# The second MLP of a decoder trunk in one written order on four engines, and the weight sums of the first MLP tied to its rows

## The chip, the cores and the metric

One NeuronCore of one Trainium2 chip runs the whole program. The metric is device time in microseconds (us) from launch to end of one execution, median over runs. Engines: TensorE (PE in the profile, PEld its weight loads), VectorE (DVE), ScalarE (ACT), GpSimd (POOL), and SyncE (SP), which issues loads.

## The reference, cut to what matters

Two layers work on 272 tokens (16 meta tokens and 256 others) of width 2048. Layer 0 mixes with RWKV-7, layer 1 with gated linear attention (GLA); after each stands a squared-ReLU MLP with 8192 hidden columns:

```python
def sq_relu_mlp(x, w1, w2):
    h = jax.nn.relu(x @ w1)
    return (h * h) @ w2
# in each layer i
h = h + mix_out                      # RWKV-7 (i = 0) or GLA (i = 1)
h = h + sq_relu_mlp(rms_norm(h, norm_mlp[i]), mlp_w1[i], mlp_w2[i])
# at the end
return rms_norm(h, norm_f)[:, N_META:]
```

All data are float32. The kernel computes each large product in three passes: a weight tile `raw` is split into `hi` (a rounded copy, by ScalarE) and `lo = raw - hi` (by VectorE), the activations likewise, and hi·hi, hi·lo and lo·hi are accumulated.

## The kernel before

The program is one straight line of stages: RWKV, the first MLP (`mlp`), GLA, the second MLP (`mlp1`). Where nothing else is said, a scheduler places each engine's instructions at compile time, by its own estimate of when their inputs are ready and by a priority; on the chip each engine then runs its list strictly in that order. `manual_schedule(engines=...)` instead puts the listed engines' instructions in the order in which the program states them. `high_priority(offset=2000)` lets the scheduler pull an instruction ahead of others.

**First MLP** (`mlp`, layer 0). The hidden columns come in 4 blocks (`NHB`) of 2048. `up(b)` makes 16 rows of 128 hidden columns, `down(b)` adds 16 rows of 128 output columns; `up(1)` runs before `down(0)`, and so on: 128 rows. A row is two weight tiles of 128x1024 (512 KB), each loaded by SP (L134), split by ScalarE (L142) and VectorE (L143), and used by 24 matmuls (L165 to L167). Three `raw` buffers and two `hi`/`lo` pairs.

**The weight sums** (`differences`). The second MLP's down product forms most of its 2x2-block products by seven products instead of eight (Strassen in Winograd's form), for six of the eight pairs of hidden rows (`FAST`). That wants three sums of weight quarters, made ahead of time: for each of 48 units (4 blocks, 2 halves of the output columns, 6 pairs) GpSimd fetches three 128x512 quarters into free `x` tiles (L329), VectorE forms three sums (L334 to L336), GpSimd stores them to the DRAM tensor `diff` (L342). The 51 steps are called between the rows of `mlp` (`paced`), store of unit u-3, fetch of u, sums of u-2 in each; nothing in the data ties a step to its row.

**Second MLP** (`mlp1`). For each block b: rows (`up`, 16 of them, two weight tiles each, 16 times a 512-wide and a 256-wide matmul, L405 and L406, into a PSUM bank `own[0]`, in a few rows another), and units (`down(b, g)`, g = output half, 8 pairs p each). A fast unit loads three tiles: A (two quarters), B (two stored sums), E (a quarter and a sum); VectorE makes a fourth, half-size operand A - B (`raw4`, L490), and seven products of three matmuls follow (L448 to L450). The two other pairs load two tiles and do eight products. After a row, ScalarE and VectorE join the two halves of the bank (L208, L209), apply the squared ReLU (L409, L414), form four sums `F` for fast pairs, and split the result into `HS` or `HC` (L426, L427). After p = 6 and p = 7 the seven banks are added into `htok`. PE's order is written by hand: rows and units alternate; VectorE, ScalarE and SP go by the scheduler, loads and splits at high priority. There are five `raw` buffers and four `hi`/`lo` pairs:

```python
def load(parts):                       # L368
    with tc.high_priority(offset=2000):
        raw = self.t(pool, [P, 1024], "raw", self.raw_bufs if pool is self.wp else 2)
        for to, src in parts:
            nc.sync.dma_start(raw[:, to], src)
        return split(pool, raw, 1024)  # L377: ScalarE cast L380, VectorE subtract through tt, L356
```

All of `mlp1`'s VectorE tensor-tensor operations show as L356 (the helper `tt`); the tiles tell them apart.

Of the kernel before, what the change touches and what calls it, by code (L numbers as in the profile page):

```python
# [56 lines left out]
class Kern:  # L57
# [203 lines left out]
    def mlp(self, layer, x, rstd, hres, off, done):  # L261
# [3 lines left out]
        with ExitStack() as es:  # L265
            hp = es.enter_context(tc.tile_pool(name=f"hid{layer}", bufs=1, side="right", reuse_waits="tile"))

            def up(b):
                hid = []
                for f in range(KT):  # L270
# [23 lines left out]
            pre = iter(())  # L294
            if layer == 0:
                pre = self.paced(self.differences(), 2 * NHB * KT - 8)
# [11 lines left out]
    def paced(self, steps, n):  # L308
        steps = list(steps)
        done = 0  # L310
        for i in range(n):
            while done < (i + 1) * len(steps) // n:
                steps[done]()
                done += 1
            yield

    def differences(self):
# [3 lines left out]
        held = {}  # L321

        def fetch(u):
            b, g, i = units[u]
            w = self.operands(b, g, FAST[i])
            held[u] = [self.t(self.xp, [P, 2, T], "x", KT, F32R).bitcast(F32).rearrange("p s t -> p (s t)")[:, :512]
                       for _ in range(3)]
            for x, k in zip(held[u], (0, 3, 2)):
                nc.gpsimd.dma_start(x, w[:, k])  # L329

        def form(u):
            x11, x12, x22 = held[u]
            tt = nc.vector.tensor_tensor
            tt(out=x22, in0=x22, in1=x12, op=ALU.subtract)  # L334
            tt(out=x12, in0=x12, in1=x11, op=ALU.subtract)
            tt(out=x11, in0=x11, in1=x22, op=ALU.add)  # L336

        def store(u):
            b, g, i = units[u]
            t2, t1, t3 = held.pop(u)  # L340
            for x, k in ((t1, 0), (t3, 1), (t2, 2)):
                nc.gpsimd.dma_start(self.diff[b, g, i][:, k], x)  # L342

        def step(u):
            if u >= 3:
                store(u - 3)
            if u < len(units):
                fetch(u)
            if 2 <= u < len(units) + 2:
                form(u - 2)  # L350

        return [lambda u=u: step(u) for u in range(len(units) + 3)]

    def mlp1(self, x, rstd):
        nc, tc, ap = self.nc, self.tc, self.ap
        tt = lambda o, a, b, op: nc.vector.tensor_tensor(out=o, in0=a, in1=b, op=op)  # L356
        w1, hres, rs = ap["mlp_w1_1"], self.hres, rstd[:, :SEQ]
# [5 lines left out]
        tmp = [flat[:, D + 512 * i : D + 512 * i + 512] for i in range(4)]  # L363
        ssq = self.t(hp, [P, 2, 4], "ssq")
        sum3 = self.t(hp, [P, 2], "sum3")
        pools = [self.wp, hp]

        def load(parts):  # L368
            with tc.high_priority(offset=2000):
                pool = pools.pop(0)  # L370
                pools.append(pool)
                raw = self.t(pool, [P, 1024], "raw", self.raw_bufs if pool is self.wp else 2)
                for to, src in parts:
                    nc.sync.dma_start(raw[:, to], src)
                return split(pool, raw, 1024)

        def split(pool, raw, n):  # L377
            hi = self.t(pool, [P, n], "hi" if n == 1024 else "hi4", self.hi_bufs, F32R)
            lo = self.t(pool, [P, n], "lo" if n == 1024 else "lo4", self.hi_bufs, F32R)
            nc.scalar.copy(hi, raw)  # L380
            tt(lo, raw, hi.bitcast(F32), ALU.subtract)
            return raw, hi, lo
# [3 lines left out]
        hid, parts = {}, {}  # L386

        def turn(i):
# [5 lines left out]
            nc.scalar.copy(htok[:, t, 512 * q : 512 * q + 512], pt)  # L394

        def up(b, f, at=0):
            ps = own[at]
            wide, one = ps.rearrange("p (s t a) -> p s t a", s=2, a=2), self.pairs(ps[:, :SEQ])
            for i in range(2):
                hi, lo = load([(slice(0, 1024), w1[b * KT + f, i])])[1:]  # L400
                for j in range(8):
                    kt = 8 * i + j
                    ws = slice(j * P, (j + 1) * P)
                    xt = x[kt][:, :, :SEQ].rearrange("p s (a t) -> p s t a", a=2)
                    nc.tensor.matmul(wide, hi[:, ws], xt, start=kt == 0, stop=False)  # L405
                    nc.tensor.matmul(one, lo[:, ws], xt[:, 0], start=False, stop=kt == KT - 1)  # L406
            c = self.joined(hp, (self.back(ps[:, :SEQ]), self.back(ps[:, SEQ:])))
            z = self.t(hp, [P, SEQ], "z", 2)
            nc.vector.scalar_tensor_tensor(out=self.two(z), in0=c, scalar=0.0, in1=self.two(rs), op0=ALU.max, op1=ALU.mult)  # L409
            p, k = f // 2, f % 2  # L410
            if k == 0:
                parts[p] = self.t(hp, [P, 8, P], "F", 2)
            F = parts[p]
            nc.scalar.activation(F[:, 2 * k : 2 * k + 2].rearrange("p a t -> p (a t)"), z, AF.Square)  # L414
            if k == 0:
                return
            x21, x11, x22, x12, s1, s2, s3, s4 = (F[:, i] for i in range(8))
            if p in FAST:
                tt(s1, x21, x22, ALU.add)
                tt(s3, x11, x21, ALU.subtract)  # L420
                tt(s2, s1, x11, ALU.subtract)
                tt(s4, x12, s2, ALU.subtract)
                src, H = F[:, 1:], self.t(hp, [P, 2, 7, P], "HS", len(FAST), F32R)
            else:
                src, H = F[:, :4], self.t(hp, [P, 2, 4, P], "HC", KT // 2 - len(FAST), F32R)
            nc.scalar.copy(H[:, 0], src)  # L426
            tt(H[:, 1], src, H[:, 0].bitcast(F32), ALU.subtract)  # L427
            hid[p] = H

        def final(t, q, late=False):  # L430
            h, i = htok[:, t, 512 * q : 512 * q + 512], q
            sq = self.t(hp, [P, 512], "fsq", 2)
            nc.scalar.activation(sq, h, AF.Square, accum_out=ssq[:, t, i : i + 1])
# [3 lines left out]
        one, two, both = slice(0, 512), slice(512, 1024), slice(0, 1024)  # L437
        t1, u2, u3, u4 = tmp
        add = lambda o, a, c: tt(o, a, c, ALU.add)

        def down(b, g):
            C = {(t, f): htok[:, t, 1024 * g + 512 * f : 1024 * g + 512 * f + 512] for t in range(2) for f in range(2)}
            begun = set()
            end = b == NHB - 1

            def product(at, X, hi, lo, ws, last, first=False):
                wh, wl, o = self.weave(hi[:, ws]), self.weave(lo[:, ws]), self.pairs(own[at])
                nc.tensor.matmul(o, X[0], wh, start=first or at not in begun, stop=False)  # L448
                nc.tensor.matmul(o, X[0], wl, start=False, stop=False)  # L449
                nc.tensor.matmul(o, X[1], wh, start=False, stop=last)  # L450
                begun.add(at)

            def evacuate(i):
                if i == 1:
                    nc.scalar.copy(t1, own[1])
                elif i == 6:
                    add(u2, own[6], t1)
                elif i == 7:
                    add(u3, own[7], u2)
                elif i == 5:  # L460
                    add(u4, own[5], u2)
                    add(C[0, 1], own[5], C[0, 1])
                elif i == 0:
                    add(C[0, 1], own[0], C[0, 1])
                    if end and g == 1 and p == KT // 2 - 1:
                        final(0, 3, True)
                elif i == 2:
                    add(C[1, 0], own[2], C[1, 0])
                    if end and g == 1:
                        final(1, 2, True)  # L470
                elif i == 3:
                    add(C[1, 1], own[3], C[1, 1])
                    if end and g == 1:
                        final(1, 3, True)
                elif i == 4:
                    add(C[0, 0], own[4], C[0, 0])
                    if end and g == 1:
                        final(0, 2, True)

            for p in range(KT // 2):  # L480
                w, H = self.operands(b, g, p), hid[p]
                if p in FAST:
                    d = self.diff[b, g, FAST.index(p)]
                    op = lambda i: (H[:, 0, i], H[:, 1, i])
                    A = load([(both, w[:, :2])])
                    B = load([(both, d[:, 1:])])
                    E = load([(one, w[:, 2]), (two, d[:, 0])])
                    with tc.high_priority(offset=2000):
                        r4 = self.t(hp, [P, 512], "raw4", 1)
# [1187 lines left out]
```

## Time and profile before

| | before |
|---|---|
| runs | 2631.57, 2612.95, 2621.63 us |
| median | 2621.63 us |
| the profiled execution | 2621.7 us, its span 2619.9 us |
| busy in the span | PE 2413.9, PEld 2239.0, DVE 1832.4, ACT 1335.9, POOL 167.9 us |
| moved by DMA | 550.93 MB, mean 210 GB/s |
| mean granted TensorE clock | 0.967 |

The stages in the span: RWKV to about 605 us, first MLP to about 1397, GLA to 1786, second MLP to 2606, then the final norm and the output. A row of a stretch of time gives, after its length, the busy time (and instructions begun) of PE, PEld, DVE, ACT and POOL, the granted clock, the DMA engines' mean busy share and GB/s. A row of a wait gives total us, how often, and the longest. A row of a group of instructions gives count, busy time and mean ns of one, then the idle time before them. A timeline row gives start, duration, engine, line and tiles.

### The profile page before, as it was taken

Reading aid. Unit: us, or ns where it says so; the run is one execution under the profiler, and the core shown is the slowest. Engines: PE = TensorE matmul, PEld = TensorE weight load, DVE = VectorE, ACT = ScalarE, POOL = GpSimd, SP = SyncE. Lnnn points to the kernel's source line nnn. Section 1 sums busy time; section 2 is a strip of 40 time slices with the busy share of each in tenths; the row PEclk is TensorE's granted clock in tenths of the full one; section 3 lists DMA queues with packets and bytes.
Section 4 is the critical chain, followed back from the end, with each engine's and each line's share of the span. In section 5 each row is a group of like instructions: output and inputs, shape, how many; then the busy total and the mean of one; then the engine's idle time right before and its main releaser. Section 6 shows DMA issues by size and latency. Waiting matters only on the chain. (4 is left out here: it accounts for less than half of the span.)

```text
span 2619.9 us, 48317 instructions
## 1 busy us (share of the span) xinstructions
PE 2413.9 (92%) x19205; PEld 2239.0 (85%) x19205; DVE 1832.4 (70%) x3025; ACT 1335.9 (51%) x2075; POOL 167.9 (6%) x325
## 2 busy tenths in 40 slices
PE   9999999988887999999999999999888888979887
PEld 8888887887777999999999999998777777868765
DVE  8779869587766555555567777776676766766767
ACT  6477455554333345344355555555554445545544
POOL 0000000024555000000000000000000000000000
PEclk9999999998999999999999999999998989989899
DMA  6478745379999655555566555555656646656564
GB/s 210 154 234 281 220 137 160 88 248 351 393 391 382 229 190 191 189 192 187 192 200 206 178 168 163 171 200 199 198 198 199 202 165 215 200 182 196 186 209 159
DMA packets 194178, 550.93 MB, mean 210 GB/s; under 512 B 40160, under 2 KB 55776, under 8 KB 193824
## 3 DMA queue, kind: packets, MB, share of 16 engines
q1 hardware_dynamic: 170912, 472.33, 54.6%
q0 software_dynamic: 23040, 75.52, 7.8%
q8 instruction: 150, 2.46, 0.4%
q14 instruction: 76, 0.62, 0.1%
HBM read 493.89 MB, written 52.17 MB: 208 GB/s over the span
## 5 line engine op out<-in xcount | busy, mean ns | idle before, releaser
L142 ACT CAST hi<-raw 128x1024 fp32r<-128x1024 f32 (+1 forms) x562 | 526.2, 947 | 638.8 <-PE pj L166 494.4
L143 DVE TENSOR_TENSOR lo<-raw,hi 128x1024 fp32r<-128x1024 f32 (+1 forms) x562 | 613.2, 1100 | 286.5 <-ACT hi L142 282.6
L167 PE MATMUL pj<-x,lo 128*128 128x272 f32 (+1 forms) x2560 | 727.4, 284 | 59.8 <-DVE lo L143 59.6
L165 PE MATMUL pj<-x,hi 128*128 128x272 f32 (+1 forms) x2560 | 737.7, 288 | 4.6 <-DVE r L566 3.9
L166 PE MATMUL pj<-x,hi 128*128 128x272 f32 (+1 forms) x2560 | 723.0, 282 | 1.4 <-DVE x L242 1.4
L167 PEld LDWEIGHTS pj<-x,lo 128*128 128x128 f32 x2560 | 493.5, 193 | 69.0 <-DVE lo L143 68.5
L165 PEld LDWEIGHTS pj<-x,hi 128*128 128x128 f32 x2560 | 493.6, 193 | 17.9 <-issue 9.8
L380 ACT CAST hi<-raw 128x1024 fp32r<-128x1024 f32 (+1 forms) x352 | 339.3, 986 | 313.7 <-DVE raw L356 82.5
L166 PEld LDWEIGHTS pj<-x,hi 128*128 128x128 f32 x2560 | 493.7, 193 | 4.2 <-DVE x L242 1.6
L356 DVE TENSOR_TENSOR lo<-raw,hi 128x1024 fp32r<-128x1024 f32 (+1 forms) x352 | 394.5, 1148 | 130.0 <-ACT hi L380 129.0
L405 PE MATMUL pj<-x,hi 128*128 128x512 f32 x896 | 323.0, 406 | 46.4 <-DVE cj L209 29.5
L165 PE MATMUL pj<-h,hi 128*128 128x272 f32 x1024 | 285.8, 279 | 1.0 <-ACT hi L142 1.0
L167 PE MATMUL pj<-h,lo 128*128 128x272 f32 x1024 | 285.9, 279 | 0.8 <-DVE lo L143 0.8
L166 PE MATMUL pj<-h,hi 128*128 128x272 f32 x1024 | 285.7, 279 | 0.0
L406 PE MATMUL pj<-x,lo 128*128 128x256 f32 x896 | 257.0, 287 | 5.1 <-DVE lo L356 4.9
L405 PEld LDWEIGHTS pj<-x,hi 128*128 128x128 f32 x896 | 180.6, 202 | 80.8 <-ACT hi L380 29.9
L165 PEld LDWEIGHTS pj<-h,hi 128*128 128x128 f32 x1024 | 193.5, 189 | 1.2 <-ACT hi L142 1.2
L167 PEld LDWEIGHTS pj<-h,lo 128*128 128x128 f32 x1024 | 193.5, 189 | 1.1 <-DVE lo L143 1.0
L166 PEld LDWEIGHTS pj<-h,hi 128*128 128x128 f32 x1024 | 193.5, 189 | 0.0
L406 PEld LDWEIGHTS pj<-x,lo 128*128 128x128 f32 x896 | 182.6, 204 | 11.2 <-DVE lo L356 10.1
L342 POOL DMA_DIRECT2D diff<-x x144 | 78.3, 545 | 534.6 <-DVE x L334 464.4
L329 POOL DMA_DIRECT2D x<-w_d x144 | 77.9, 542 | 129.7 <-DMA diff<-x 56.4
(369 smaller groups left out, 3583.8 us busy)
## 6 DMA issues: line engine op xcount, KB each, us to landing
raw<-mlp_w_d SPq DMA_DIRECT2D x384, 512.0 KB, 4.4
raw<-gla_in_d SPq DMA_DIRECT2D x98, 512.0 KB, 3.8
raw<-w_rkv_d SPq DMA_DIRECT2D x80, 512.0 KB, 4.3
raw<-w_d SPq DMA_DIRECT2D x80, 512.0 KB, 4.8
x<-w_d POOLq DMA_DIRECT2D x144, 256.0 KB, 7.7
diff<-x POOLq DMA_DIRECT2D x144, 256.0 KB, 7.2
raw<-diff SPq DMA_DIRECT2D x48, 512.0 KB, 4.4
raw<-gla_o_d SPq DMA_DIRECT2D x32, 512.0 KB, 4.3
```

Of the source, the lines that this page charges most:

```text
L142: nc.scalar.copy(hi[:, h], raw[:, h])
L143: nc.vector.tensor_tensor(out=lo[:, h], in0=raw[:, h], in1=hi[:, h].bitcast(F32), op=ALU.subtract)
L165: nc.tensor.matmul(out, hi[:, ws], xh, start=first, stop=False)
L166: nc.tensor.matmul(out, hi[:, ws], xl, start=False, stop=False)
L167: nc.tensor.matmul(out, lo[:, ws], xh, start=False, stop=last)
L329: nc.gpsimd.dma_start(x, w[:, k])
L342: nc.gpsimd.dma_start(self.diff[b, g, i][:, k], x)
L356: tt = lambda o, a, b, op: nc.vector.tensor_tensor(out=o, in0=a, in1=b, op=op)
L380: nc.scalar.copy(hi, raw)
L405: nc.tensor.matmul(wide, hi[:, ws], xt, start=kt == 0, stop=False)
L406: nc.tensor.matmul(one, lo[:, ws], xt[:, 0], start=False, stop=kt == KT - 1)
```

## The change

In `mlp`, `tick` takes the place of `paced`: after each row it runs the steps that are due over 118 rows, and hands them a two-element slice `mark` of what the row has just written (`z` in an up row, `hres` in a down row). GpSimd copies `mark` into the edge of two of the three tiles before it fetches them, and once more ahead of a unit's sums, whose first subtract is widened to read it.

In `mlp1` the work becomes a list, `stream`, with one slot per weight tile (two per row, four per fast unit, the fourth without a load, two per other unit). One loop states slot after slot what all four engines do: first what is due before (`before`: joins, sums, bank additions of earlier slots), then the split of the tile three slots ahead (`AHEAD = 3`), a new load for each `raw` buffer that comes free, then what is due behind (`behind`: squares, casts), then the slot's matmuls. PE, DVE, ACT and SP are all in the manual order, nothing has a priority. `raw4` is made right after the split of B, from two buffers instead of one. Rows and units keep PE's alternation. The order of the products within a unit changes (1 2 | 6 7 | 5 3 | 4 by tile), and the other units go tile by tile. The odd ones of the first ten rows, and row 9 of each later block, use bank 4.

```diff
-                    next(pre, None)
+                    tick(z[:, :2])
...
-                    next(pre, None)
+                    tick(hres[:, f, off : off + 2])
-            if layer == 0:
-                pre = self.paced(self.differences(), 2 * NHB * KT - 8)
+            steps = self.differences()
+            rows, made = 2 * NHB * KT - 10, [0, 0]
+            def tick(mark):
+                made[0] += 1
+                while made[1] < min(len(steps), made[0] * len(steps) // rows):
+                    steps[made[1]](mark)
+                    made[1] += 1
...
             for x, k in zip(held[u], (0, 3, 2)):
-                nc.gpsimd.dma_start(x, w[:, k])
+                if k != 2:
+                    nc.gpsimd.tensor_copy(x[:, 511:513], mark)
+                nc.gpsimd.dma_start(x[:, body], w[:, k])
...
-            tt(out=x22, in0=x22, in1=x12, op=ALU.subtract)
+            nc.gpsimd.tensor_copy(x22[:, 512:514], mark)
+            tt(out=x22[:, wide], in0=x22[:, wide], in1=x12[:, wide], op=ALU.subtract)
...
+                later(slot + 1, join)
+                later(slot + 1, square, True)
...
+                if p in FAST:
+                    later(slot + 2, sums)
...
+                later(slot + 2, lambda: nc.scalar.copy(H[:, 0], src), True)
+                later(slot + 3, lambda: tt(H[:, 1], src, H[:, 0].bitcast(F32), ALU.subtract))
...
+                stream.append(([(both, w[:, :2])], pe([(1, 0, one), (2, 2, two)])))
+                stream.append(([(both, d[:, 1:])], pe([(6, 4, two), (7, 5, one)])))
+                stream.append(([(one, w[:, 2]), (two, d[:, 0])], pe([(5, 3, two), (3, 6, one)])))
+                stream.append((None, pe([(4, 1, one)])))
...
+        def load():
+            while loads and free[0]:
+                i = loads.pop(0)
+                free[0] -= 1
...
+                for to, src in stream[i][0]:
+                    nc.sync.dma_start(raws[i][:, to], src)
+        def split(i):
...
+            nc.scalar.copy(hi, raw)
+            tt(lo, raw, hi.bitcast(F32), ALU.subtract)
...
+            if is_b:
+                fourth[i + 2] = self.t(hp, [P, 512], "raw4", 2)
+                tt(fourth[i + 2], raws[i - 1][:, two], raw[:, two], ALU.subtract)
+                free[0] += 2
+            elif stream[i][0] and not is_a:
+                free[0] += 1
+            load()
+        engines = {mybir.EngineType.PE, mybir.EngineType.DVE, mybir.EngineType.Activation, mybir.EngineType.SP}
+        with tc.manual_schedule(engines=engines):
+            load()
+            done = 0
+            for i in range(len(stream) + 8):
+                for f in before.pop(i, []):
+                    f()
+                while done < min(len(stream), i + AHEAD + 1):
+                    split(done)
+                    done += 1
+                for f in behind.pop(i, []):
+                    f()
+                if i < len(stream):
+                    stream[i][1](sets.pop(i), i)
+                if i == 20:
+                    nc.sync.dma_start(nf, ap["nf"].to_broadcast([P, D]))
```

More of the change, by code (lines that the diff above doesn't have):

```diff
@@ L341, in store, with step @@
             for x, k in ((t1, 0), (t3, 1), (t2, 2)):
-                nc.gpsimd.dma_start(self.diff[b, g, i][:, k], x)
-        def step(u):
+                nc.gpsimd.dma_start(self.diff[b, g, i][:, k], x[:, body])
+        def step(u, mark):
             if u >= 3:
@@ L347, in step @@
             if u < len(units):
-                fetch(u)
+                fetch(u, mark)
             if 2 <= u < len(units) + 2:
-                form(u - 2)
-        return [lambda u=u: step(u) for u in range(len(units) + 3)]
+                form(u - 2, mark)
+        return [lambda mark, u=u: step(u, mark) for u in range(len(units) + 3)]
     def mlp1(self, x, rstd):
@@ L362, in mlp1, with later @@
         nf = flat[:, :D]
-        tmp = [flat[:, D + 512 * i : D + 512 * i + 512] for i in range(4)]
+        t1, u2, u3, u4 = (flat[:, D + 512 * i : D + 512 * i + 512] for i in range(4))
         ssq = self.t(hp, [P, 2, 4], "ssq")
         sum3 = self.t(hp, [P, 2], "sum3")
[L366 to L382, printed above, removed]
         own = {i: f() for i, f in zip((1, 2, 7, 6, 5, 3, 4, 0), (self.pu, self.pu, self.ptr, self.ptr, self.pm, self.pry,
                                                                 self.pj, self.pj))}
-        hid, parts = {}, {}
+        hid, parts, before, behind = {}, {}, {}, {}
+        one, two, both = slice(0, 512), slice(512, 1024), slice(0, 1024)
+        stream, fourth, AHEAD = [], {}, 3
+        def later(slot, f, after=False):
+            (behind if after else before).setdefault(slot, []).append(f)
         def turn(i):
@@ L393, in turn, with row @@
                                     self.ident)
-            nc.scalar.copy(htok[:, t, 512 * q : 512 * q + 512], pt)
-        def up(b, f, at=0):
+            return lambda: nc.scalar.copy(htok[:, t, 512 * q : 512 * q + 512], pt)
+        def row(b, f, at=0, extra=None):
             ps = own[at]
-            wide, one = ps.rearrange("p (s t a) -> p s t a", s=2, a=2), self.pairs(ps[:, :SEQ])
-            for i in range(2):
[L400 to L428, printed above, removed]
@@ new lines, in row, with pe, run @@
+            wide, narrow = ps.rearrange("p (s t a) -> p s t a", s=2, a=2), self.pairs(ps[:, :SEQ])
+            def pe(i):
+                def run(w, slot):
+                    hi, lo = w
+                    for j in range(8):
+                        kt = 8 * i + j
+                        ws = slice(j * P, (j + 1) * P)
+                        xt = x[kt][:, :, :SEQ].rearrange("p s (a t) -> p s t a", a=2)
+                        nc.tensor.matmul(wide, hi[:, ws], xt, start=kt == 0, stop=False)
+                        nc.tensor.matmul(narrow, lo[:, ws], xt[:, 0], start=False, stop=kt == KT - 1)
+                    if i == 1:
+                        post(slot)
+                        if extra is not None:
+                            later(slot + 1, turn(extra), True)
+                return run
@@ new lines, in row, with post, join, square @@
+            p, k = f // 2, f % 2
+            def post(slot):
+                if k == 0:
+                    parts[p] = self.t(hp, [P, 8, P], "F", 2)
+                F = parts[p]
+                c, z = self.t(hp, [P, SEQ], "cj", 2), self.t(hp, [P, SEQ], "z", 2)
+                x21, x11, x22, x12, s1, s2, s3, s4 = (F[:, i] for i in range(8))
+                def join():
+                    nc.scalar.copy(self.two(c), self.back(ps[:, SEQ:]))
+                    add(self.two(c), self.back(ps[:, :SEQ]), self.two(c))
+                    nc.vector.scalar_tensor_tensor(out=z, in0=c, scalar=0.0, in1=rs, op0=ALU.max, op1=ALU.mult)
+                def square():
+                    nc.scalar.activation(F[:, 2 * k : 2 * k + 2].rearrange("p a t -> p (a t)"), z, AF.Square)
+                def sums():
+                    add(s1, x21, x22)
+                    tt(s3, x11, x21, ALU.subtract)
+                    tt(s2, s1, x11, ALU.subtract)
+                    tt(s4, x12, s2, ALU.subtract)
+                later(slot + 1, join)
+                later(slot + 1, square, True)
+                if k == 0:
+                    return
+                if p in FAST:
+                    later(slot + 2, sums)
+                    src, H = F[:, 1:], self.t(hp, [P, 2, 7, P], "HS", len(FAST), F32R)
+                else:
+                    src, H = F[:, :4], self.t(hp, [P, 2, 4, P], "HC", KT // 2 - len(FAST), F32R)
+                later(slot + 2, lambda: nc.scalar.copy(H[:, 0], src), True)
+                later(slot + 3, lambda: tt(H[:, 1], src, H[:, 0].bitcast(F32), ALU.subtract))
+                hid[p] = H
@@ L438, in mlp1, with unit @@
[L438 to L441 removed]
+        def unit(b, g, p):
             C = {(t, f): htok[:, t, 1024 * g + 512 * f : 1024 * g + 512 * f + 512] for t in range(2) for f in range(2)}
[L443 to L448, printed above, removed]
[L449 to L517 removed]
@@ L542, in mlp1 @@
[L542 to L559 removed]
+            w = self.operands(b, g, p)
@@ new lines, in pe, with run, empty @@
+            def pe(k):
+                def run(w, slot):
+                    H = hid[p]
+                    order = ((2, 3, 4, 0), (2, 3, 0, 4) if end else (0, 2, 3, 4))[k]
+                    for at in order:
+                        h, ws = {2: (1, one), 0: (0, two), 3: (1, two), 4: (0, one)}[at]
+                        product(at, (H[:, 0, 2 * k + h], H[:, 1, 2 * k + h]), w, ws, at == 0 and k == 0,
+                                k == 1 and (at == 0 or last))
+                    if k == 0:
+                        return
+                    outs = {2: (1, 0), 3: (1, 1), 0: (0, 1), 4: (0, 0)}
+                    for n, at in enumerate(order):
+                        if at == 0 or last:
+                            def empty(at=at):
+                                add(C[outs[at]], own[at], C[outs[at]])
+                                if last and b == NHB - 1 and end:
+                                    final(outs[at][0], 2 * g + outs[at][1], True)
+                            later(slot + 1 + n // 2, empty)
+                    if last and b == NHB - 1 and g == 0:
+                        for n in range(4):
+                            later(slot + 4 + n, lambda n=n: final(n // 2, n % 2))
+                return run
@@ new lines, in unit @@
+            for k in range(2):
+                stream.append(([(both, w[:, 2 * k : 2 * k + 2])], pe(k)))
+        for f in range(10):
+            row(0, f, (0, 4)[f % 2], f if f < 8 else None)
+        for b in range(NHB):
+            for p in range(KT // 2):
+                unit(b, 0, p)
+                if p < 6:
+                    row(b, 10 + p)
+            for p in range(KT // 2):
+                if b < NHB - 1:
+                    row(b + 1, p)
+                unit(b, 1, p)
+            if b < NHB - 1:
+                row(b + 1, 8)
+                row(b + 1, 9, 4)
```

156 lines of the change are left out of this document (71 added, 85 removed).

## The prediction

> **What bounds the kernel now.** I read the slices first, to see where TensorE falls below full, then the table of stretches, then the waits within two of them, then timelines for the pitch of single instructions. The stretches:
>
> ```profile
> 545.00:610.00 65.00, 56.02 (x456) 53.76 (x455) 55.99 (x113) 34.19 (x69) 23.10 (x44) 1.00 0.88 293
> 610.00:860.00 250.00, 198.66 (x1488) 192.81 (x1487) 174.90 (x247) 89.69 (x124) 130.16 (x242) 0.92 1.01 386
> 1110.00:1360.00 250.00, 250.00 (x2159) 249.85 (x2158) 143.28 (x170) 112.95 (x140) 1.64 (x3) 1.00 0.58 193
> 1783.00:2620.00 837.00, 712.16 (x3494) 612.24 (x3492) 587.95 (x778) 420.98 (x555) 0.00 (x0) 0.92 0.58 193
> ```
>
> The third row is the first MLP undisturbed: 2159 matmuls in 250 us. The second is the same code with POOL busy on the weight sums: 1488, so 250 x (1 - 1488/2159) = 78 us are lost there. The first, the end of RWKV, loses 65 - 56 = 9 us while POOL already works. Loss together: **87 us**. The waits of 520 to 860 us and the loads of 620 to 860 say by what:
>
> ```profile
> DVE x L334 <- DMA x<-w_d: 65.9, 33, 4.9
> PE pj L167 <- DVE lo L143: 54.3, 29, 4.7
> raw<-mlp_w_d SPq DMA_DIRECT2D x61, 512.0 KB, 7.2
> ```
>
> VectorE stands at a sum whose quarters have not landed, and the weight subtract behind it comes late. PE waits for `lo`, hardly for `hi`: weight loads landing in 7.2 us were still in time.
>
> In the second MLP no engine is full (the fourth row), so it is bound by order. Its waits, and its first and last matmul:
>
> ```profile
> DVE lo L356 <- ACT hi L380: 128.3, 100, 4.5
> DVE raw L356 <- DMA raw<-diff: 38.3, 25, 3.0
> PE pj L448 <- DVE cj L209: 37.9, 10, 4.5
> DVE raw L356 <- DMA raw<-w_d: 37.2, 16, 4.3
> PE pj L405 <- DVE cj L209: 29.5, 12, 4.2
> PE pj L405 <- DVE htok L356: 14.4, 3, 5.6
> ...
> 1785.94 0.38 PE L405 MATMUL pj<-x,hi 128*128 128x512 f32 x1
> 2605.92 0.38 PE L450 MATMUL pry<-hi,HC 128*128 128x512 f32 x1
> ```
>
> VectorE waits 75.5 us at `raw4` for B's load; the joins `cj` that free PE's bank queue behind it. PE takes 2606.3 - 1785.9 = **820 us**.
>
> **The change, second MLP.** PE's matmuls stay, so I price its floor from its pitch where it runs freely:
>
> ```profile
> 2050.01 0.38 PE L405 MATMUL pu<-x,hi 128*128 128x512 f32 x1
> 2053.61 0.38 PE L405 MATMUL pu<-x,hi 128*128 128x512 f32 x1
> 2053.94 0.38 PE L448 MATMUL pt<-hi,HS 128*128 128x512 f32 x1
> 2057.61 0.38 PE L450 MATMUL pj<-hi,HS 128*128 128x512 f32 x1
> ```
>
> Eleven wide-narrow pairs lie between the first two: 0.327 us each, so a row (16) takes 5.24. Seventeen matmuls lie between the others: 0.216, so a fast unit (21) takes 4.54 and another (24) 5.18. 64 rows, 48 and 16 units: 335 + 218 + 83 = 636 us, 638 with the transposes (2, estimated at 32 x 0.06). So 182 of the 820 us are waits and slow clock.
>
> VectorE is the next limit:
>
> ```profile
> L356 DVE TENSOR_TENSOR lo<-raw,hi 128x1024 fp32r<-128x1024 f32 x303 | 364.2, 1221 | 127.2 <-ACT hi L380 126.3
> L356 DVE TENSOR_TENSOR raw<-raw,raw 128x512 f32<-128x512 f32 x48 | 33.2, 692 | 75.5 <-DMA raw<-diff 38.3 <-DMA raw<-w_d 37.2
> L356 DVE TENSOR_TENSOR lo<-raw,hi 128x512 fp32r<-128x512 f32 x48 | 32.9, 685 | 2.1 <-ACT hi L380 2.1
> L356 DVE TENSOR_TENSOR F<-F 128x128 f32<-128x128 f32 x96 | 27.8, 289 | 9.1 <-ACT F L414 7.7
> L409 DVE SCALAR_TENSOR_TENSOR z<-cj,acc 128x256 f32<-128x256 f32 x64 | 27.0, 422 | 1.4
> L356 DVE TENSOR_TENSOR HS<-F,HS 128x896 fp32r<-128x896 f32 x24 | 26.1, 1088 | 4.2 <-ACT HS L426 4.2
> L209 DVE TENSOR_TENSOR cj<-pj,cj 128x256 f32<-128x256 f32 x56 | 23.4, 418 | 4.2 <-ACT cj L208 4.2
> L356 DVE TENSOR_TENSOR htok<-htok,hres 128x512 f32<-128x512 f32 x36 | 23.2, 685 | 0.0
> 2598.31 2.36 DVE L356 TENSOR_TENSOR lo<-raw,hi 128x1024 fp32r<-128x1024 f32 x2 [0.61 <-ACT hi L380]
> ```
>
> Two `lo` take 2.36 us, not 2.44: 0.08 of each lies over the next. So `lo` costs 1.14, a 512-wide one 0.61, HS 1.01, the four F 0.84, cj with z 0.84. A row of a fast pair is 2.28 + 0.84 + (0.84 + 1.01)/2 = 4.05, of a slow pair 3.43; a fast unit 3 x 1.14 + 2 x 0.61 = 4.64, a slow one 2.28; the bank additions of one output half (13) 7.9. By stretches, PE against VectorE: half 0 of a block (6 rows, 8 units) 69.0 against 63.4; half 1 with 8 rows 79.5 against 71.5; the last half, without rows, 37.6 against 40.3. PE leads everywhere but in the last: 638 + 2.7 = 641 us.
>
> To that come stalls. At the end of half 0, PE's last two units take 9.7 us, VectorE's work of that time 4.6 + 2.3 of splits, 1.4 of row 15 and 12 additions of 0.61: 15.6, some 6 behind. Splits three slots ahead hide that for the weights, but the next row wants bank 0, whose addition stands last in that work: 4 us, three times; 1.5 us three times at the end of half 1, where a row lies between and row 8 follows. Together 16.5. The start stalls as now, 7 (below). For waits that a strict order itself makes (ScalarE's square behind `z`, its cast behind the square) nothing in this trace has a row; nothing at least, 75 at most (the second rival); I take 20, by the start's 7 and a hand-over's 4 nearer the low end. Sum 641 + 16.5 + 7 + 20 = 685, **135 us less**.
>
> SP's loads move into the same order. They need 160.55 MB in 685 us, 234 GB/s:
>
> ```profile
> raw<-mlp_w_d SPq DMA_DIRECT2D x124, 512.0 KB, 4.5
> q1 hardware_dynamic: 170912, 472.33, 54.6%
> ```
>
> Over the span this queue moved 472 MB at 54.6% busy, so about 330 GB/s would be full, and a load is stated five of the 352 slots ahead (5 x 685/352 = 9.7 us) against 4.5 to land: hidden. Uncovered it is the last rival. The `nf` load at slot 20 waits for transposes that slot 17 has ended: nothing queues behind it. The 13.6 us from last matmul to span's end stay.
>
> The start, from the stretches, shows what a wait does to the clock:
>
> ```profile
> 1790.00:1795.00 5.00, 2.30 (x7) 1.82 (x8) 3.68 (x3) 2.92 (x4) 0.00 (x0) 0.73 0.58 206
> 1795.00:1800.00 5.00, 5.00 (x22) 4.46 (x20) 0.85 (x2) 1.24 (x3) 0.00 (x0) 0.59 0.60 203
> 1800.00:1805.00 5.00, 5.00 (x34) 4.63 (x33) 2.65 (x3) 2.64 (x4) 0.00 (x0) 1.00 0.33 102
> ```
>
> PE idles 2.7 us, the granted clock falls to 0.59, and the next 5 us do 22 matmuls instead of 34; 39 of 68 missing in 10 us would be 5.7, rounded up to 7 for its edges. [...]
>
> **The change, first MLP.** The same 288 transfers and 144 sums now go 51 steps over 118 rows; a row takes two tiles of 2.78 us:
>
> ```profile
> 1118.40 1.05 ACT L142 CAST hi<-raw 128x1024 fp32r<-128x1024 f32 x1 [1.73 <-PE pj L166]
> 1118.51 0.44 DVE L215 TENSOR_TENSOR hres<-pj,hres 128x272 f32<-128x272 f32 x1 [0.59 <-PE pj L167]
> 1119.48 1.23 DVE L143 TENSOR_TENSOR lo<-raw,hi 128x1024 fp32r<-128x1024 f32 x1 [0.52 <-ACT hi L142]
> 1121.18 1.05 ACT L142 CAST hi<-raw 128x1024 fp32r<-128x1024 f32 x1 [1.73 <-PE pj L166]
> L329 POOL DMA_DIRECT2D x<-w_d x144 | 77.9, 542 | 129.7 <-DMA diff<-x 56.4 <-DVE r L566 43.5 <-DMA x<-w_d 25.8
> L917 POOL COPY WC<-W 128x4 f32<-128x4 f32 x16 | 5.4, 338 | 199.5 <-ACT W L899 199.5
> ```
>
> So a step comes each 13 us, a unit's quarters land two steps before their sums, and the 65.9 us of VectorE's wait go; 75.5 MB in 656 us are 115 GB/s beside the weights' 193, under the 386 that the second stretch carried. What is late next is VectorE's sum itself. The new copies (three a step, 0.34 each by L917; 144 in all, 49 us of POOL's free time) put a chain into it: mark, copy, fetch, copy, fetch, fetch, copy: 3 x 0.34 + 3 x 0.54 = 2.64 us of POOL before the first sum may start, with `lo`, joins and `z` queued behind it on VectorE, and PE behind `lo`. If the scheduler puts that sum ahead of the next `lo`: the mark is written 0.55 after the cast's start, the sum ends at 0.55 + 2.64 + 0.61 = 3.80, `lo` at 4.94, and PE wants it at 2.78 + 0.23: 1.95 late, 48 times, 94 us. If behind it, the sums fall into VectorE's gaps (1.55 us in every second tile): 0. I take 0.69, the length of one sum, since one in front of `lo` is what a fixed order easily leaves: 33 us. Gain 87 - 33 = **54**.
>
> **Sum**: 2621.7 (the profiled execution; the median is 2621.63) - 135 - 54 = **2433 us**, 7.2% less.
>
> **Rivals.** VectorE waits behind POOL: 94 instead of 33, the first MLP gains nothing, 2621.7 - 135 + 7 = 2494. For: the schedule already misjudged POOL by up to 4.9 us. Against: `lo` has priority. 0.14.
>
> Only the waits on transfers go in the second MLP (75.5), while the strict order keeps VectorE waiting for ScalarE (the 128): 2621.7 - 75 - 54 = 2492. For: that wait is the largest. Against: three slots ahead is about 6 us, more than its longest, 4.5. 0.13.
>
> The copies do not hold the steps back: 2621.7 - 135 = 2487; against it, each first sum reads a copy. 0.02.
>
> POOL's copy and VectorE's subtract block each other: one `lo` of 1.22 more in the chain, 3.17 x 48 = 152 given for 87: 2552. [...] 0.03.
>
> Everything lies under TensorE: sums hidden wholly (87), stalls of 17 in all (655 us, 165 less): 2370. 0.05.
>
> Slower: loads. Five `raw` buffers, less one half the time for A, which waits for B: some 4.3 in flight. A tile's period is (landing + 2.2 of split) / 4.3; now it is 820/304 = 2.70, so from 9.4 us of landing on this is slower, and at 11 it is 3.07 x 304 = 933: 2621.7 + 113 - 54 = 2681. Against: 7.2 was the median in the busiest stretch, at 386 GB/s. 0.03.
>
> **Numbers.** My forecast, 0.60, by itself 2385 to 2480 (stalls of 0 to 60, sums 0 to 60 given back). The range 2385 to 2510 takes in both rivals near 2490 and leaves out the last three and the edges, about 0.18. A run of this kernel tells about 1% (26 us) from no change. Faster by more: all but the last rival and some of its neighbours, 0.95; same 0.02; slower 0.03.
>
> **What would show it.** Right: POOL busy from about 620 to 1260 us in even steps, some 2150 matmuls in each 250 us there, no VectorE wait for x<-w_d; second MLP's PE 660 to 710 us, clock near 1, waits at `raw4` gone, the longest left at bank 0 after p = 7. Wrong: L334 waiting for POOL; `hi` waiting for `raw`; VectorE waiting for `hi` over 100 us.

## The result and the profile after

| | before | after |
|---|---|---|
| median of runs | 2619.24 us | 2452.62 us |
| ratio | | 0.936, 95% interval 0.932 to 0.940 |
| span of the profiled execution | 2619.9 us | 2450.8 us |
| first MLP and GLA end, second MLP begins on PE | 1785.9 us | 1739.9 us |
| last matmul ends | 2608.2 us | 2436.9 us |
| second MLP on PE | 822 us | 697 us |

The forecast was 2433 us, range 2385 to 2510. Of the 169 us between the two spans, 46 were won ahead of the second MLP and 125 in it, and the stretch behind the last matmul grew by 2 (11.7 us before, 13.9 after). The prediction took a matmul that starts at 2605.92 for the last one of the kernel before; these are the last ones, before and after:

```profile
2607.86 0.38 PE L450 MATMUL pj<-hi,HC 128*128 128x512 f32 x1
2436.47 0.38 PE L459 MATMUL pj<-hi,HC 128*128 128x512 f32 x1
```

So its 820 us for the second MLP are 822, and its 13.6 us behind it 11.7.

The stretches of the changed kernel (columns as before):

```profile
545.00:610.00 65.00, 64.50 (x554) 64.22 (x553) 52.86 (x102) 39.62 (x77) 0.00 (x0) 1.00 0.55 179
610.00:860.00 250.00, 240.53 (x2012) 235.15 (x2011) 160.35 (x207) 110.23 (x144) 70.93 (x162) 1.00 0.85 286
860.00:1110.00 250.00, 241.91 (x2025) 236.59 (x2024) 160.60 (x204) 105.19 (x129) 73.63 (x162) 1.00 0.85 289
1737.00:2451.00 714.00, 663.15 (x3493) 586.88 (x3492) 587.86 (x778) 418.57 (x555) 0.00 (x0) 0.97 0.68 224
```

The end of RWKV is full again, and POOL's work lies evenly over the first MLP: 2012 matmuls where there were 1488, but not the 2159 of the undisturbed stretch. What is left there shows in the waits between 600 and 1330 us, and in the landing of the weight loads:

```profile
ACT hi L142 <- DMA raw<-mlp_w_d: 192.2, 87, 4.1
...
PEld pj L167 <- DVE lo L143: 34.4, 63, 1.0
PE pj L167 <- DVE lo L143: 20.3, 41, 0.8
...
DVE x L335 <- POOL x L334: 5.9, 12, 1.8
...
raw<-mlp_w_d SPq DMA_DIRECT2D x215, 512.0 KB, 5.8
```

VectorE no longer stands at a fetch, and almost never at POOL. ScalarE now stands at weight loads, which it did for 56 us before, in the same window.

The second MLP's waits, from 1735 us on, and the hand-over from half 0 to half 1 of block 2 (counted from 0) on PE and VectorE:

```profile
DVE lo L357 <- ACT hi L552: 77.6, 87, 3.0
...
PE pj L396 <- DVE htok L357: 21.4, 10, 5.1
...
PE pj L457 <- DVE cj L357: 6.5, 3, 2.2
...
PE pu L457 <- DVE htok L357: 5.5, 1, 5.5
```

```profile
2215.02 0.38 PE L459 MATMUL pj<-hi,HC 128*128 128x512 f32 x1
2220.46 0.76 PE L396 MATMUL pj<-x,hi 128*128 128x512 f32 x1 [5.06 <-DVE htok L357]
2221.01 0.42 PE L397 MATMUL pj<-x,lo 128*128 128x256 f32 x1
2221.23 0.63 PE L396 MATMUL pj<-x,hi 128*128 128x512 f32 x1
```

```profile
2216.08 1.29 DVE L357 TENSOR_TENSOR htok<-htok,hres 128x512 f32<-128x512 f32 x2
2217.29 1.22 DVE L357 TENSOR_TENSOR lo<-raw,hi 128x1024 fp32r<-128x1024 f32 x1
2218.42 1.29 DVE L357 TENSOR_TENSOR htok<-htok,hres 128x512 f32<-128x512 f32 x2
2219.62 0.69 DVE L357 TENSOR_TENSOR htok<-pj,htok 128x512 f32<-128x512 f32 x1
```

No wait of VectorE at `raw4` is left (75.5 us before), and its wait for `hi` fell from 128 us to 78. PE stands 5 us until the addition `htok<-pj` has freed bank 0, behind four additions that read no bank. Then its first wide-narrow pair takes 0.77 us and the next ones 0.65 each, instead of 0.327.

The second MLP from its first matmul to its last, before and after:

```profile
1785.90:2608.30 822.40, 709.26 (x3476) 609.58 (x3474) 582.78 (x767) 415.36 (x541) 0.00 (x0) 0.93 0.59 193
1739.90:2436.90 697.00, 660.25 (x3476) 584.22 (x3474) 581.15 (x763) 412.43 (x539) 0.00 (x0) 0.97 0.69 227
```

PE idled 113 us of the 822 and idles 37 of the 697. Against the floor of 638 that the prediction works out, its busy time holds, by estimate, 71 us lost in pace before and 22 after. So 76 of the 125 us are waits and 49 are pace.

### The profile page after: what moved, and what is told of

The parts are those of the page before. It is cut to its first block, busy times and chain, and to the rows that moved or that the text cites. A ratio compares the mean times of both kernels' runs of the same rounds, so it can differ in the third digit from the quotient of the medians.

```text
span 2450.8 us, 48648 instructions
## 1 busy us (share of the span) xinstructions
PE 2356.0 (96%) x19205; PEld 2196.8 (90%) x19205; DVE 1829.5 (75%) x3025; ACT 1332.0 (54%) x2075; POOL 206.5 (8%) x469
## 4 chain that ended last, share of the span: by engine, by line
PE 59%; DVE 18%; DMA 12%; ACT 5%; issue 4%; POOL 2%; SPq 0%; ACTq 0%; DVEq 0%; POOLq 0%
DMA raw<-mlp_w_d 11%; PE pj L396 9%; PE pj L167 9%; PE pj L165 9%; PE pj L166 9%; DVE lo L143 5%; PE pj L397 4%; ACT hi L142 3%; PE pj L198 2%; DVE lo L357 2%; DVE htok L357 1%; POOL x L329 1%; PE pj L199 1%; PE pu L457 1%; PE pu L458 1%
## 5 line engine op out<-in xcount | busy, mean ns | idle before, releaser
L142 ACT CAST hi<-raw 128x1024 fp32r<-128x1024 f32 (+1 forms) x562 | 526.1, 947 | 644.3 <-PE pj L166 364.3
L143 DVE TENSOR_TENSOR lo<-raw,hi 128x1024 fp32r<-128x1024 f32 (+1 forms) x562 | 613.5, 1101 | 336.5 <-ACT hi L142 330.4
L167 PE MATMUL pj<-x,lo 128*128 128x272 f32 (+1 forms) x2560 | 719.5, 281 | 16.3 <-DVE lo L143 15.5
L165 PE MATMUL pj<-x,hi 128*128 128x272 f32 (+1 forms) x2560 | 728.7, 285 | 3.2 <-ACT hi L142 1.6
L166 PE MATMUL pj<-x,hi 128*128 128x272 f32 (+1 forms) x2560 | 713.8, 279 | 0.5 <-DVE x L242 0.5
L167 PEld LDWEIGHTS pj<-x,lo 128*128 128x128 f32 x2560 | 484.8, 189 | 25.8 <-DVE lo L143 24.8
L357 DVE TENSOR_TENSOR lo<-raw,hi 128x1024 fp32r<-128x1024 f32 x352 | 396.5, 1148 | 80.5 <-ACT hi L552 78.5
L552 ACT CAST hi<-raw 128x1024 fp32r<-128x1024 f32 x352 | 338.6, 986 | 142.9 <-PE pj L396 77.8
L396 PE MATMUL pj<-x,hi 128*128 128x512 f32 x1024 | 347.6, 389 | 22.6 <-DVE htok L357 21.4
L397 PE MATMUL pj<-x,lo 128*128 128x256 f32 x1024 | 282.2, 276 | 0.8 <-DVE lo L357 0.8
L396 PEld LDWEIGHTS pj<-x,hi 128*128 128x128 f32 x1024 | 196.8, 192 | 55.0 <-issue 16.3
L397 PEld LDWEIGHTS pj<-x,lo 128*128 128x128 f32 x1024 | 199.7, 195 | 2.2 <-DVE lo L357 1.1
L198 PE MATMUL pj<-x,hi 128*128 128x512 f32 x256 | 84.1, 382 | 0.1
```

The costliest lines, as they stand in the source:

```text
L142: nc.scalar.copy(hi[:, h], raw[:, h])
L143: nc.vector.tensor_tensor(out=lo[:, h], in0=raw[:, h], in1=hi[:, h].bitcast(F32), op=ALU.subtract)
L165: nc.tensor.matmul(out, hi[:, ws], xh, start=first, stop=False)
L166: nc.tensor.matmul(out, hi[:, ws], xl, start=False, stop=False)
L167: nc.tensor.matmul(out, lo[:, ws], xh, start=False, stop=last)
L397: nc.tensor.matmul(narrow, lo[:, ws], xt[:, 0], start=False, stop=kt == KT - 1)
```

## The experiments

**The two halves apart** (e1, e2): the unchanged stage is put back from the kernel before.

```diff
# e1: mlp and differences of the kernel before
-                    tick(z[:, :2])
+                    next(pre, None)
...
# e2: mlp1 of the kernel before
```

> The second MLP in its new order, the first MLP and its weight sums as before. If the two parts of the change add up, the second MLP's TensorE stretch is 697 us as in the changed kernel (820 before), the second MLP starts at about 1786 us, and the time is 2619 - 123 = 2496 us. Rival: the parts interact (the new second MLP depends on what the first leaves, by clock or by loads), then the stretch differs from 697 by more than 10 us.

> The weight sums tied to the rows, the second MLP as before. Additive: the second MLP starts 46 us earlier, at 1740, takes 820 us as before, 2619 - 46 = 2573 us. Rival: interaction, more than 10 us off.

Measured: e1 2495.9 us (ratio 0.953, 0.950 to 0.956), the second MLP 698 us on PE; e2 2571.8 us (0.982, 0.978 to 0.986: a gain, but not clear of 2%), the second MLP begins at 1734.7. So the parts add up: 123 and 47 us by time. One thing was off: the old second MLP took 833 us in e2, 11 more than before, in the longest of that kernel's four runs (2581.1). Small differences between executions are to be reckoned with here. In six profiles with the first MLP of the changed kernel (after, after_again, e2, e3, e4, e7) the second began at 1739.9, 1737.2, 1734.7, 1737.6, 1740.8 and 1725.3. The new second MLP is steadier: 697.0 to 698.4 us on PE in six profiles (after, after_again, e1, e5, e10, e11).

**Bank 7, and later additions** (e3, e4).

```diff
# e3
-                    row(b + 1, p)
+                    row(b + 1, p, 0 if p else 7)
...
-                row(b + 1, 8)
+                row(b + 1, 8, 7)
# e4 (the lines are cut at their ends)
-  later(slot + 3, lambda: (add(C[1, 0], C[1, 0], t1), ...
+  later(slot + (3 if end else 6), lambda: (add(C[1, 0], C[1, 0], t1), ...
-  later(slot + 4, lambda: (add(C[0, 1], C[0, 1], u3), ...
+  later(slot + (4 if end else 7), lambda: (add(C[0, 1], C[0, 1], u3), ...
```

> The changed kernel, but the first row after each output half goes to bank 7, free since p = 6, instead of bank 0. Theory: TensorE's wait at bank 0 (31 us of weight-load idle at L396 for htok, and the slow clock behind it) is what the backlog of additions costs; 20 to 35 us less than the changed kernel's 2453, so 2418 to 2433. Rival: VectorE is 6 us behind there in any case and TensorE only waits one slot later, for lo: less than 8 us gained.

> The changed kernel, but four of the additions after p = 6 (those that read no bank) are stated three slots later, behind the additions that free banks 0 and 2. Theory: each hand-over waits 2 x 0.61 to 4 x 0.61 us less, seven times, 8 to 17 us, and some slow clock with it: about 2438. Rival: the work is only moved and stalls the next unit instead: 2453 within 5.

Measured: e3 2443.0 us (0.933, 0.930 to 0.936), e4 2441.2 (0.932, 0.929 to 0.935); second MLP 680 and 685 us on PE against 697. By time alone neither interval is clear of the changed kernel's (0.932 to 0.940); the stretches are, against the six profiles above. PE's groups in e3:

```profile
L396 PE MATMUL pj<-x,hi 128*128 128x512 f32 x928 | 310.1, 385 | 7.4 <-DVE htok L357 6.2 <-ACT hi L552 1.2
L457 PE MATMUL pt<-hi,HS 128*128 128x512 f32 x96 | 37.2, 388 | 7.7 <-DVE cj L357 7.7
```

The 21.4 us at L396 fell to 6.2, but 7.7 came up one unit later, at bank 7, three times: VectorE's backlog is real, and the first unit meets it. e3 stands between the theory (20 to 35) and the rival (under 8); in its own stretch it gave 17, and the wait in two pieces stays short. e4 gave what was expected, 12 in its stretch: PE's three longest waits fell from 5.06 to 2.65 us each.

**A lead of two slots instead of three** (e7).

```diff
-        stream, fourth, AHEAD = [], {}, 3
+        stream, fourth, AHEAD = [], {}, 2
```

> The changed kernel with weight tiles split two slots ahead instead of three (same loads, same buffers). Theory: the lead carries VectorE's backlog over the short slots of a unit and the hand-overs; without a third of it 20 to 60 us are lost, 2473 to 2513, with waits for lo. Rival: what helps is the written order alone, the lead of two is enough: 2453 within 8.

Measured: 2486.1 us (0.952, 0.949 to 0.955), the second MLP 746 us on PE, 49 more (some 34 by time, as its second MLP began 15 us earlier). Its waits there:

```profile
PEld pj L397 <- DVE lo L357: 24.3, 21, 1.3
PEld pj L396 <- ACT hi L552: 24.3, 21, 1.6
```

Both halves of a split come late, 21 times each. So the lead, not the written order alone, holds 49 of the 125 us. How the other 76 divide between the places of splits, joins and additions, the second `raw4` buffer and the new order of products, no run separates.

**`raw4` without B's load, in the kernel before** (e6).

```diff
-  tt(r4, A[0][:, two], B[0][:, two], ALU.subtract)
+  tt(r4, A[0][:, two], A[0][:, one], ALU.subtract)
```

> The kernel before, but the half-size operand raw4 is made from the two quarters of A alone, so it no longer waits for B's load; the products that use it come out other. If the wait of VectorE for that load (75 us) is what the change took away in the second MLP, this gives most of its 123 us: 2500 to 2540. If the order of splits, joins and additions as a whole is, little: 2585 to 2615, the joins still late.

Measured: 2587.6 us (0.991, 0.988 to 0.993), the second MLP 783 us on PE: 39 of the 125 us in the stretch, 27 by time. The wait did not go, it moved to A's load:

```profile
DVE raw L356 <- DMA raw<-w_d: 72.7, 43, 5.3
...
PE pj L448 <- DVE cj L209: 40.8, 10, 5.6
...
PE pj L405 <- DVE cj L209: 18.4, 16, 2.2
```

75.5 us of waiting at `raw4` are 72.7 now, and PE still waits 59 us for the joins, where it waited 67. VectorE comes to `raw4` too early for either input; one input less does not mend an order. So e6 doesn't tell what the wait for B alone was worth.

**What the first MLP still loses** (e5, e11, e13).

```diff
# e5: in form (three lines cut at their ends)
-            nc.gpsimd.tensor_copy(x22[:, 512:514], mark)
-            tt(out=x22[:, wide], ...
-            tt(out=x12[:, body], ...
-            tt(out=x11[:, body], ...
# e11: step becomes two, over the same 118 rows
+        def first(u, mark):
+            if u < len(units):
+                fetch(u, mark)
+        def second(u, mark):
+            if u >= 3:
+                store(u - 3)
+            if 2 <= u < len(units) + 2:
+                form(u - 2, mark)
# e13
-                nc.gpsimd.dma_start(x[:, body], w[:, k])
+                nc.gpsimd.dma_start(x[:, :256], w[:, k, :256])
... (the sums read the residual; the second MLP loads weight quarters for the sums)
-                nc.gpsimd.dma_start(self.diff[b, g, i][:, k], x[:, body])
+                nc.gpsimd.dma_start(self.diff[b, g, i][:, k, :256], x[:, :256])
```

> The changed kernel without VectorE's three weight sums and without the copy ahead of them: the fetched quarters are stored as they are, so the second MLP multiplies by other weights; every transfer stays. The first MLP still loses some 47 us against its undisturbed pace. Theory (weight loads land late while a step's six transfers run): the loss stays, matmuls per 250 us at 860 to 1110 stay near 2025 (2159 undisturbed), time within 10 us of 2453. Rival (the sums stand in front of the weight subtract on VectorE, as predicted, 33 us): 2410 to 2425 and over 2100 matmuls.

> The changed kernel, but a unit's fetch and another unit's sums and stores go to different rows (102 half steps over the 118 rows instead of 51 steps), so that three transfers come at a time instead of six. If bursts are what delays the weight loads: half of the 47 us comes back, 2425 to 2440. If it is the total number of bytes beside the weights: no change, 2453 within 8.

> The changed kernel with as many transfers for the weight sums, but half as long (256 of 512 columns); VectorE's three sums have their full length and take their inputs from the residual, and one small subtract of two columns reads the mark; the second MLP loads weight quarters in the place of the sums. If bytes beside the weight loads are what the first MLP loses its 47 us to: over 25 us come back, 2420 to 2428, landing of the weight loads near 5. If VectorE's sums are: under 10 us, 2443 or more.

The changed kernel stood beside e13 once more:

> The changed kernel once more, so that the next three stand beside it on the same chip: 2453 us by the first measurement, ratio to before 0.936. Its first MLP is read for how much the 47 us of loss differ between executions.

It took 2450.6 us (0.936, 0.934 to 0.939). e5 took 2436.7 us (0.933, 0.930 to 0.936) and 2088 matmuls between 860 and 1110 us; e11 took 2437.8 (0.932, 0.930 to 0.935), with 2068. Both intervals overlap that of the changed kernel. The nearest row to set them against is that of e7, which has the first MLP of the changed kernel and was measured beside them:

```profile
860.00:1110.00 250.00, 244.81 (x2059) 240.41 (x2058) 165.00 (x209) 108.33 (x135) 75.07 (x168) 1.00 0.87 295
```

Against it e5 brings back 29 matmuls and e11 9; their second MLPs begin at 1720.5 and 1723.2, where that of e7 begins at 1725.3. So e5 returns little, and e11 by itself shows no return. (Without the sums a store starts as soon as its fetch has landed: POOL stood at `x<-w_d` ahead of its stores for 264.9 us in 126 waits, so e5 moves transfers as well.) e13 decides: 2419.8 us (0.924, 0.922 to 0.926), 31 less than the changed kernel beside it. Its stretch, its waits and its landings:

```profile
860.00:1110.00 250.00, 249.91 (x2130) 247.77 (x2129) 173.70 (x239) 113.41 (x143) 73.70 (x173) 1.00 0.77 247
```

```profile
ACT hi L142 <- DMA raw<-mlp_w_d: 10.1, 5, 2.7
PEld pj L167 <- DVE lo L143: 8.1, 31, 1.2
```

```profile
raw<-mlp_w_d SPq DMA_DIRECT2D x226, 512.0 KB, 4.6
```

With all 144 sums at full length on VectorE and all 288 transfers at half length, 2130 of 2159 matmuls are there. Most of the loss is the bytes beside the weight loads: they land in 5.8 us with them, in 4.6 with half of them. What is still missing, 29 matmuls or 3.4 us in 250, is the most that the sums can cost in e13.

The sums do stand in front of `lo`, as the prediction had it. In the changed kernel:

```profile
707.54 1.05 ACT L142 CAST hi<-raw 128x1024 fp32r<-128x1024 f32 x1 [0.34 <-PE pj L166]
708.68 0.69 DVE L336 TENSOR_TENSOR x<-x,x 128x512 f32<-128x512 f32 x1
709.29 1.22 DVE L143 TENSOR_TENSOR lo<-raw,hi 128x1024 fp32r<-128x1024 f32 x1
```

`hi` is there at 708.59, and `lo` starts at 709.29, behind the sum. Read that way, from the end of `hi` to the start of `lo`, the sums hold `lo` back 19 times in that stretch of e13, 12.7 us in all. Little of it reaches TensorE.

**Only the fetches tied** (e10).

```diff
-            nc.gpsimd.tensor_copy(x22[:, 512:514], mark)
-            tt(out=x22[:, wide], in0=x22[:, wide], in1=x12[:, wide], op=ALU.subtract)
+            tt(out=x22[:, body], in0=x22[:, body], in1=x12[:, body], op=ALU.subtract)
```

> The changed kernel without the copy ahead of the sums: only the fetches are tied to rows. If the tie of the fetch is what matters: 2453 within 8, the sums still two steps after their fetch. If the scheduler then puts a sum right behind its fetch again, VectorE stands waiting for x<-w_d as before and 30 to 60 us are lost in the first MLP: 2480 to 2510.

Measured: 2611.0 us (0.997, 0.995 to 0.999); the second MLP begins at 1901.7, 164 us later than in the changed kernel beside it. Waits and a stretch of the first MLP:

```profile
PEld pj L167 <- DVE lo L143: 133.9, 42, 4.4
DVE x L334 <- DMA x<-w_d: 125.8, 42, 4.2
PE pj L167 <- DVE lo L143: 125.4, 42, 4.2
```

```profile
860.00:1110.00 250.00, 207.12 (x1635) 204.10 (x1635) 131.33 (x165) 83.14 (x100) 52.28 (x120) 0.94 0.70 237
```

The second theory holds, at more than its price: 160 us, where 30 to 60 were set down. VectorE waits at the sum of the quarters fetched last, about 3 us in each step, over the whole stage instead of a third of it. Pacing the fetches alone is worse than no pacing: 1786 before, 1902 here.

**All three mends together** (e12).

> The changed kernel with the half steps of e11, bank 7 of e3 and the later additions of e4 together. e3 and e4 gave some 10 us each, e11 some 10 to 15. If the three stalls are separate: 30 less than the changed kernel, 2415 to 2425. If bank 7 and the later additions cure the same wait: 15 to 20 less, 2430 to 2438.

Measured: 2414.1 us (0.9225, 0.920 to 0.925), 36 less than the changed kernel beside it (0.936, 0.934 to 0.939). The second MLP begins at 1727.3 and takes 676 us on PE. Bank 7 and the later additions together gave 21 there, against 17 and 12 apart: partly the same wait. The half steps of e11 begin it 10 us earlier than in the changed kernel beside it (1737.2); e7's 1725.3 shows that this much can also be a difference between executions. It is the fastest version here.

## Why the prediction was right, step by step

**What bounds it.** That the two stages lose for two unconnected reasons held: 125 and 46 us in the profile of the change, 123 and 47 by time when apart.

**Second MLP**, 685 forecast, 697 measured. The floor of 638 and VectorE's balance stood: VectorE was busy 588 us before and after. Of the 59 us over the floor PE idles 37 and loses 22 in pace. Two terms of the sum were off and nearly cancel, which is luck. The hand-overs, priced at 16.5, cost 33: the 21.4 at L396 (three waits of 5.06 at bank 0, forecast as 4; three of 1.46 behind the unit with p = 3, which the sum didn't have; four short ones), 6.5 at L457 (three, inside the last unit of half 1, which wants bank 0 before the row in it is joined) and 5.5 (one, at the start of the last half, where no row lies between). What the strict order makes by itself, put at 20, is at most the 4 us of idleness that are left. So the 12 us that the forecast missed are in the last term: the pace. The sum had it for the start alone (in the 7); with 22 lost in all, at a mean granted clock of 0.97, it was too small. No run shows the 0.06 us that the floor takes for a transpose: before and after, four of them take 0.35 us (at 1838.32 and at 1748.38), so 32 would be 2.8 us where 2 stand.

**First MLP**, a gain of 54 forecast, 46 measured. The size was near by luck, the step was wrong. "What is late next is VectorE's sum itself" held for the order: one sum stands in front of `lo` and holds it back by about its length. It failed for the price: in e13 this was 12.7 us of lateness in 250 us, and TensorE lost 3.4 of them at most. What TensorE waits for next is the weight load. The prediction set it aside because 115 + 193 GB/s lie under the 386 that the second stretch carried, and because 7.2 us of landing had seemed in time; but in that stretch TensorE ran at 1488/2159 of its pace and needed its tiles later. So 41 us were given back, most of them to loads, where 33 had been set down for sums. Whether bursts matter besides the bytes (six transfers come together) is open: e11 shows no clear return. Two of the signs came out against the prediction here: some 2150 matmuls were to be in each 250 us, and there are 2012 and 2025; and `hi` waiting for `raw`, listed as a sign of being wrong, came to 192 us.

**The rivals.** VectorE behind POOL: the waits for the new copy came to 5.9 us, 12 times for 48 copies; the first sum of a step stands behind a subtract in VectorE's order, and the other 36 times it found the copy done. Only the transfers' waits go: both kinds of wait fell, the one at `raw4` from 75.5 us to nothing and the one for `hi` from 128 to 78; e6, which moved the former instead of removing it, can't price this rival. The copies don't hold: given 0.02 and 2487; they hold, and the one ahead of the sums is needed, since leaving it out costs nearly the whole change (e10); whether the two ahead of the fetches are needed too, no run shows. Loads in a strict order: they landed in 4.5 to 5.5 us at 226 GB/s, far from 9.4. POOL and VectorE blocking each other: POOL's side of it is there (last section: 31 of 48 copies end with a subtract, after up to 1.25 us), but the mean `lo` of the first MLP takes 1.22 us as before.

## What to carry to other kernels

An engine that works through a fixed list waits wherever the list was made with a wrong idea of arrival: VectorE stood 65.9 us at fetched quarters before and not at all after. Tie such work to the pace of its stage by a dependence, and tie the consumer too: pacing the fetches alone was worse here than no pacing (the second MLP began at 1902 us, against 1786). When the order is written by hand, give the splits of weights a lead as long as the worst backlog (a slot less cost 49 us of the second MLP in e7), and state first what frees a bank that the next product wants (12 us in e4). Count the pace lost behind each wait, not only the wait: by estimate 2.8 us behind one of 5.06. The cost of transfers beside a stage bound by compute was here the lateness of that stage's own loads, which landed in 5.8 us and, beside half the bytes, in 4.6: compare the landing time with the slack at full pace, not at the pace of the disturbed stretch. And an operation that is late on an engine costs only what reaches the engine that bounds the stage: in e13 `lo` was late by 12.7 us, and TensorE lost 3.4 at most.

## What the runs showed of the hardware

The TensorE clock behind a wait, in the changed kernel:

```profile
2215.00:2220.00 5.00, 0.40 (x2) 0.00 (x0) 5.00 (x8) 1.04 (x1) 0.00 (x0) 0.93 0.74 273
2220.00:2225.00 5.00, 4.54 (x14) 3.94 (x15) 3.84 (x6) 0.00 (x0) 0.00 (x0) 0.50 0.24 61
2225.00:2230.00 5.00, 5.00 (x27) 4.49 (x26) 2.06 (x4) 1.94 (x3) 0.00 (x0) 0.89 0.51 181
```

After these 5 us of idleness the granted clock was 0.50 for the next 5 us. A pair then took 0.65 us instead of 0.327. In the 4.54 busy us of the second row 14 matmuls begin where 28 would at full pace, and in the third row 27 where 30 would; so by estimate this wait cost some 2.8 us more than its length.

POOL's copies of two elements, ahead of the fetches (L328) and ahead of the sums (L334), and one of the latter beside VectorE's subtract:

```profile
L334 POOL COPY x<-z 128x2 f32<-128x2 f32 x25 | 14.1, 562 | 0.0
L328 POOL COPY x<-z 128x2 f32<-128x2 f32 x54 | 9.5, 208 | 297.0 <-DVE z L274 297.0
...
718.72 0.89 POOL L334 COPY x<-z 128x2 f32<-128x2 f32 x1
718.34 1.23 DVE L143 TENSOR_TENSOR lo<-raw,hi 128x1024 fp32r<-128x1024 f32 x1 [1.53 <-ACT hi L142]
```

The same copy takes 208 ns on average in one place and 562 in the other, and this one ends at 719.61, with the subtract that began before it (719.57). That is no accident of one row: of the 48 copies ahead of the sums, 31 take 0.23 to 1.25 us; each of these begins while a VectorE subtract with two inputs runs and ends 0.03 to 0.05 us behind it. The other 17 take 0.2 at most.
